# Loading the first norm's gain as one row, with a stream of zeros through TensorE while the tokens load

## The chip, the cores and the metric

The kernel runs on one core of a Trainium2 chip. The metric is device time in microseconds of one launch, as the median over runs. A core has five engines with queues of their own: TensorE (PE in the profile, its weight loads PEld), VectorE (DVE), ScalarE (ACT), GpSimd (POOL) and SyncE (SP), which issues the loads here.

## The reference

A decoder trunk of two layers on 256 tokens of width 1024, fp32. Each layer is a half-step SwiGLU feed-forward block, a token mixer (RWKV-7 in the first layer, sliding-window attention in the second), and another half-step feed-forward block, with a norm before and after each.

```python
def rms_norm(x, g):
    y = x * lax.rsqrt(jnp.mean(x * x, axis=-1, keepdims=True) + RMS_EPS)
    return y * g

def swiglu(x, w_in, w_out):
    gate, up = jnp.split(x @ w_in, 2, axis=-1)
    return (jax.nn.silu(gate) * up) @ w_out

for layer in range(DEPTH):
    g = norm_g[layer]
    h = h + 0.5 * rms_norm(swiglu(rms_norm(h, g[0]), ffn_w_in[layer, 0], ffn_w_out[layer, 0]), g[1])
    ...
```

The change concerns the very first step, `rms_norm(h, g[0])` of layer 0, and with it the first 36 us or so.

## The kernel before

Tokens lie on partitions in two blocks of 128, `self.h[0]` and `self.h[1]`, each 128x1024. A product with fp32 weights is made of three products in a reduced format (`mm3`, L226): the weight chunk (`wr`, 128x1024, 512 KB) is cast to a high part by ScalarE (L195), VectorE subtracts to get the low part (L201), and both lie in `W`. The activations are split the same way (`split`, L313): high part on ScalarE (L314), low part on VectorE (L315), into `xtl` (features 0 to 511) and `xth` (512 to 1023).

The start, in the order of the program:

- SP issues the load of `h[0]` (L89), of the identity (`cst`, L91), then the gain of the first norm (`gain`, L157): the row of 1024 values is read 128 times, once for each partition, 512 KB in all. Then comes the first weight chunk, `h[1]`, and more chunks. Four buffers `wr` hold raw chunks.
- For each token block, `hstat` (L285) squares the block on ScalarE (L290), `rstd` (L235) makes the factor r on VectorE (L239) and GpSimd (L242), `normed` (L294) multiplies the block with r and the gain in two halves of 512 on VectorE (L301), `transposed` (L305) turns each half with four TensorE transposes against the identity (L309), and `split` follows.
- `ffn_lead` then makes the first two blocks of the hidden layer from eight chunks (`w_in_lead`): 96 products of 512 columns, which show as L227. `ffn_main` streams the other weights (L362, L363, and L227 for the way down).

PSUM is used by banks of 128x512: six of them rotate as `bk` (`bank`), two as `bt` (`tbank`). The pools `t4` (four buffers of 128x1024) and `g2k` (fourteen of 128x512) rotate as well.

The program is written in the order above, but the order on each engine's queue comes from a scheduler that works with estimated durations; only some stages are pinned by hand. So at the start, seven products of the first token block stand ahead of the second block's transposes.

Of the kernel before, what the change touches and what calls it, by code (L numbers as in the profile page):

```python
# [16 lines left out]
P = 128  # L17
# [10 lines left out]
R_NORM = {}  # L28
# [49 lines left out]
class Trunk:  # L78
# [215 lines left out]
    def normed(self, i, r, g, xn):  # L294
        nc = self.nc
        for n in range(2):
            sl = slice(n * 512, n * 512 + 512)
            if g is None:
                nc.vector.tensor_scalar(xn[:, sl], self.h[i][:, sl], r, None, op0=ALU.mult)
            else:  # L300
                nc.vector.scalar_tensor_tensor(xn[:, sl], self.h[i][:, sl], r, g[:, sl],  # L301
                                               op0=ALU.mult, op1=ALU.mult)
        return xn

# [282 lines left out]
    def tm_core(self):  # L587
# [35 lines left out]

        acc0, todo = v_half(0, xv)
        run(todo)
        self.mix(xkm[:, :, toks[1]], 2, toks[1])
        self.tm_lora(1)
# [549 lines left out]
        for i in range(2):  # L1177
            unit.update({f"m{i}": merge(i), f"t{i}": bk_turn(i), f"y{i}": rows(i), f"bias{i}": gn_bias(i),
                         f"gate{i}": gn_gate(i), f"gn{i}": normed(i), f"yt{i}": turned(i), f"o{i}": out_proj(i),
                         f"c{i}0": chain(i, 0), f"c{i}1": chain(i, 1)})  # L1180
# [289 lines left out]
    def run(self, out):  # L1470
        nc, a = self.nc, self.a
        self.out = out
        self.tm_open()
        self.open("xt")
        self.open("sh0")
        self.tl("sh0", [P, 24])
        self.open("W1", 3)
        self.open("t4", 4)
        self.open("g2k", 14)
        self.tm_begin()  # L1480
        self.open("l1", side="right")
        self.open("W2", 5, side="right")
        self.turns = ["W1", "W2", "W2", "W1", "W2", "W2", "W1", "W2"]

        self.ffn_begin(0, None, 2, 3)
        g_pre = self.gain(R_NORM[(0, 0)])
        self.lead_chunk(0, 0)
        nc.sync.dma_start(self.h[1], a["x"][P:T, :])
        self.xt = xt = self.new_xt("xt")
        for i in range(2):  # L1490
            self.to_xt(i, self.hstat(i), [(g_pre, xt)])
        self.ffn_lead((0, 1))
        self.ffn_main()
        self.load(self.cols, a["cols"], self.mid)
        self.load(self.small, a["small"].to_broadcast([P, 272]), self.mid)
        self.load(self.cst[:, P:], a["consts"][:, P:], self.mid)
        self.tm_consts()
        g_post = self.gain(R_NORM[(0, 1)], self.mid)
        for i in range(2):
            self.tm_in(i, self.post(i, self.ffn_tail(i), g_post, True))  # L1500
        accs, g_post = self.tm_core()

        g_pre = self.gain(R_NORM[(0, 4)])
        xt = self.new_xt("xt")
        for i in range(2):
            self.to_xt(i, self.post(i, accs[i], g_post, False), [(g_pre, xt)])
        self.ffn_begin(1, xt)
        self.plan = list(P1)
        for i in range(2):
            self.ffn_lead((i,))  # L1510
        self.ffn_main()
        g_post = self.gain(R_NORM[(0, 5)], self.mid)

        self.kv_open()
        xt = self.new_xt("xt")
        xe = self.new_xt("ux", ("u", "xx"))
        self.plan = list(PKV)
        self.wkv = [self.stream(a["w_kv"][c], gains=C_GKV + 2 * c) for c in range(3)]
        for i in range(2):
            self.to_xt2(i, self.post(i, self.ffn_tail(i, self.early(i, TX1)), g_post, True), xe, xt)  # L1520
        self.ffn_begin(2, xt, 1)
        for i in range(2):
            self.kv(i, xe)
            self.ffn_lead((i,))
        self.ffn_main()
        self.att_region()
        self.ffn_main()
        g_post = self.gain(R_NORM[(1, 5)], self.mid)
        for i in range(2):
            self.post_last(i, self.ffn_tail(i), g_post)  # L1530
        for p in reversed(self.psum):
            p.release()
        self.close("W3", "W2", "ux", "kvp", "t4", "pad", "qT", "W1", "g2k", "sh2", "xt")
# [88 lines left out]
```

## Time and profile before

| what | value |
|---|---|
| median of three runs | 1058.08 us (1057.75 to 1059.89) |
| profiled execution | 1058.52 us |
| its span, first to last instruction | 1056.7 us |
| TensorE busy | 1027.6 us, 97% of the span |
| VectorE busy | 699.5 us, 66% |
| ScalarE busy | 565.3 us, 53% |
| mean granted TensorE clock | 0.996 |
| bytes read from HBM | 180.94 MB |

Busy time is the time in which the engine had work, not the time at its peak. In the lists, a line gives its start, its length, the engine, the source line, the tiles as out<-in, the shape, and in brackets how long the engine had stood idle and what ended that. A span of several instructions is merged into one line with their count (x7).

The row of the slices that gives the clock granted to TensorE shows full clock in every slice from the first on, also where no product had run yet; for the start, the pace of TensorE's own instructions says more.

### The profile page before, as it was taken

To read this page: it belongs to the slowest core of one execution; us is meant where nothing else is said; L and a number is where in the kernel's file an instruction comes from. 1 tells how busy PE (TensorE), PEld (TensorE's weight loads), DVE (VectorE), ACT (ScalarE), POOL (GpSimd) and SP (SyncE) were. 2 spreads that over 40 slices of the span, in tenths; PEclk is the share of its full clock that TensorE was granted. 3 is DMA by queue.
4 is the path that set the end of the run, shared out by engine and by line. 5 is a ranking of instruction groups with operands and counts; after the bars stand their busy time and mean duration, and the time that the engine had idled before them with its cause. 6 is when DMAs were issued, how large, how long until landed. Compare 5 with 4: busy or idle time off the path is not lost.

```text
span 1056.7 us, 16152 instructions
## 1 busy us (share of the span) xinstructions
PE 1027.6 (97%) x6264; PEld 859.3 (81%) x6264; DVE 699.5 (66%) x1125; ACT 565.3 (53%) x1014; POOL 20.5 (2%) x34
## 2 busy tenths in 40 slices
PE   6999999999999999999999999999999979999997
PEld 5888888779967887888888788888877758888885
DVE  6766655527798977766665676666658876765652
ACT  6654554355244546655455665455556755655541
POOL 0000000000000001000000000000010000000000
PEclk9999999999999999999999999999999999999999
DMA  8868665034354346766563376675535127766621
GB/s 285 248 187 279 220 193 165 23 117 141 120 167 135 122 134 207 258 199 206 194 182 122 116 268 212 209 237 189 180 104 175 41 94 254 237 214 196 183 78 40
DMA packets 52668, 183.04 MB, mean 173 GB/s; under 512 B 5744, under 2 KB 6000, under 8 KB 52464
## 3 DMA queue, kind: packets, MB, share of 16 engines
q1 hardware_dynamic: 52304, 181.49, 53.4%
q8 instruction: 49, 0.80, 0.3%
q10 hardware_dynamic: 288, 0.52, 0.1%
q14 instruction: 27, 0.22, 0.1%
HBM read 180.94 MB, written 1.05 MB: 172 GB/s over the span
## 4 chain that ended last, share of the span: by engine, by line
PE 91%; ACT 3%; DVE 3%; DMA 1%; issue 1%; POOL 0%; SPq 0%; DVEq 0%; POOLq 0%; ACTq 0%
PE bk L227 36%; PE bt L362 13%; PE bk L362 13%; PE bt L363 7%; PE bk L363 7%; PE bk L571 3%; PE bk L617 2%; PE bk L581 1%; PE bt L309 1%; PE bc L1002 1%; PE bk L1053 1%; ACT W L195 1%; PE bk L1397 1%; ACT g2k L1368 1%; DVE t L259 0%
## 5 line engine op out<-in xcount | busy, mean ns | idle before, releaser
L201 DVE TENSOR_TENSOR W<-wr,W 128x1024 fp32r<-128x1024 f32 x280 | 341.2, 1225 | 192.8 <-ACT W L195 191.9
L195 ACT CAST W<-wr 128x1024 fp32r<-128x1024 f32 x280 | 291.8, 1050 | 190.7 <-issue 96.5
L227 PE MATMUL bk<-W,g2k 128*128 128x512 f32 x1056 | 250.7, 394 | 0.0
L227 PEld LDWEIGHTS bk<-W,g2k 128*128 128x128 f32 x1056 | 196.1, 188 | 44.1
L362 PE MATMUL bk<-xtl,W 128*128 128x512 f32 x296 | 104.8, 392 | 0.0
L362 PE MATMUL bt<-xth,W 128*128 128x512 f32 x296 | 104.6, 391 | 0.0
L362 PE MATMUL bt<-xtl,W 128*128 128x512 f32 x296 | 104.4, 391 | 0.0
L362 PE MATMUL bk<-xth,W 128*128 128x512 f32 x296 | 104.4, 391 | 0.0
L363 PE MATMUL bt<-xth,W 128*128 128x256 f32 x296 | 83.3, 281 | 0.0
L363 PE MATMUL bk<-xth,W 128*128 128x256 f32 x296 | 83.2, 281 | 0.0
L363 PE MATMUL bk<-xtl,W 128*128 128x256 f32 x296 | 83.2, 281 | 0.0
L363 PE MATMUL bt<-xtl,W 128*128 128x256 f32 x296 | 83.1, 281 | 0.0
L227 PE MATMUL bk<-W,xtl 128*128 128x512 f32 x216 | 60.4, 427 | 6.4 <-ACT W L195 3.5
L362 PEld LDWEIGHTS bt<-xtl,W 128*128 128x128 f32 x296 | 55.6, 188 | 12.3 <-DVE xtl L350 0.5
L362 PEld LDWEIGHTS bk<-xtl,W 128*128 128x128 f32 x296 | 55.6, 188 | 12.2
L362 PEld LDWEIGHTS bk<-xth,W 128*128 128x128 f32 x296 | 55.6, 188 | 11.9
L362 PEld LDWEIGHTS bt<-xth,W 128*128 128x128 f32 x296 | 55.5, 188 | 11.8
L227 PEld LDWEIGHTS bk<-W,xtl 128*128 128x128 f32 x216 | 42.0, 200 | 20.0 <-ACT W L195 4.0
L363 PEld LDWEIGHTS bk<-xtl,W 128*128 128x128 f32 x296 | 55.9, 189 | 1.4
L363 PEld LDWEIGHTS bt<-xth,W 128*128 128x128 f32 x296 | 55.8, 189 | 0.1
L363 PEld LDWEIGHTS bt<-xtl,W 128*128 128x128 f32 x296 | 55.8, 189 | 0.1
L363 PEld LDWEIGHTS bk<-xth,W 128*128 128x128 f32 x296 | 55.8, 189 | 0.0
(287 smaller groups left out, 1375.7 us busy)
## 6 DMA issues: line engine op xcount, KB each, us to landing
wr<-in_w_in_dram SPq DMA_DIRECT2D x148, 512.0 KB, 3.8
wr<-in_w_out_dram SPq DMA_DIRECT2D x88, 512.0 KB, 3.6
wr<-in_w_in_lead_dram SPq DMA_DIRECT2D x28, 512.0 KB, 4.2
wr<-in_w_v_dram SPq DMA_DIRECT2D x16, 512.0 KB, 3.9
gain<-in_rows_dram SPq DMA_DIRECT2D x13, 512.0 KB, 4.5
wr<-in_w_k_dram SPq DMA_DIRECT2D x8, 512.0 KB, 4.0
wr<-in_w_r_dram SPq DMA_DIRECT2D x8, 512.0 KB, 3.5
wr<-in_w_o_dram SPq DMA_DIRECT2D x8, 512.0 KB, 4.3
```

Of the source, the lines that this page charges most:

```text
L195: self.follow(nc.scalar.copy(w[:, 0, :], raw), 0)
L201: self.follow(nc.vector.tensor_tensor(w[:, 1, :], raw, w[:, 0, :], op=ALU.subtract), 1)
L227: mm = lambda *x, **y: self.nc.tensor.matmul(*x, **y, **kw)
L309: t = self.nc.tensor.transpose(b[:, k * P:(k + 1) * P], xn[:, c:c + P], self.ident)
L362: mm(banks[j], hi[:, c0:c0 + P], xt[c][:, :, k4, :], start=(k == 0), stop=False)
L363: use[0] = mm(banks[j][:, 0:T], lo[:, c0:c0 + P], xt[c][:, 0, k4, :], start=False, stop=(k == KT - 1))
L571: self.nc.tensor.matmul(b[:, j * T:(j + 1) * T], ws[k // 4][:, c0:c0 + P], xf[:, k, :], start=(k == 0), stop=(k == KT - 1))
L581: nc.tensor.matmul(bs[j], l[:, k, j * P:(j + 1) * P], x[:, k, sl], start=(k == 0 and not e), stop=(k == KT - 1 and e == 1))
L617: mm(acc, x[:, 2 * k2 + k, :], w[:, k, :], start=(k2 + k == 0), stop=(k2 + k == 4))
L1002: mm(b[r, m * N:(m + 1) * N], W[r, v - hh * 16, :], XV[r, v, :], start=True, stop=True)
L1053: mm(out[hh][half[1 - e], m * N:(m + 1) * N], lhs, UV[part][:, hh * 16 + q, :], start=(not i and part == 0 and m == 0), stop=(part == e), ...
L1368: nc.scalar.activation(S[x], S[x], AF.Exp, bias=st[:, 1, x:x + 1], accum_out=st[:, 3, x:x + 1])
```

## The change

The gain of the first norm is loaded as a single row of 4 KB onto one partition. TensorE spreads it: a row of 128 ones as the stationary operand and the gain's row as the moving one give, in two products of 512 columns with one row of contraction, the gain on all 128 partitions, in two PSUM banks. `normed` then reads it from PSUM. Ahead of these two products stand five products of a 128x512 tile of zeros with itself, whose result nothing reads. The tiles for zeros and ones are set by VectorE.

```diff
-                nc.vector.scalar_tensor_tensor(xn[:, sl], self.h[i][:, sl], r, g[:, sl],
+                nc.vector.scalar_tensor_tensor(xn[:, sl], self.h[i][:, sl], r, g[n] if isinstance(g, list) else g[:, sl],
                                                op0=ALU.mult, op1=ALU.mult)
...
         self.ffn_begin(0, None, 2, 3)
-        g_pre = self.gain(R_NORM[(0, 0)])
+        zero, one, row = self.g2k([P, 512]), self.g2k([P, 512]), self.t4()
+        nc.vector.memset(zero, 0.0)
+        nc.vector.memset(one[0:1, 0:P], 1.0)
+        nc.sync.dma_start(row[0:1, :], a["rows"][R_NORM[(0, 0)]:R_NORM[(0, 0)] + 1, :])
+        busy = self.tbank()
+        for _ in range(5):
+            nc.tensor.matmul(busy, zero[:, 0:P], zero, start=True, stop=True)
+        g_pre = [self.bank() for _ in range(2)]
+        for n in range(2):
+            nc.tensor.matmul(g_pre[n], one[0:1, 0:P], row[0:1, n * 512:n * 512 + 512], start=True, stop=True)
         self.lead_chunk(0, 0)
         nc.sync.dma_start(self.h[1], a["x"][P:T, :])
```

## The prediction

> **What bounds the kernel now.** I read the page first, then TensorE's waits, the chain of waits over the first 16 us, and the timeline there, engine by engine.
>
> The page: the span, TensorE's line, and the shares of the chain that ended last.
>
> ```profile
> span 1056.7 us, 16152 instructions
> PE 1027.6 (97%) x6264; PEld 859.3 (81%) x6264; DVE 699.5 (66%) x1125; ACT 565.3 (53%) x1014; POOL 20.5 (2%) x34
> PE 91%; ACT 3%; DVE 3%; DMA 1%; issue 1%; POOL 0%; SPq 0%; DVEq 0%; POOLq 0%; ACTq 0%
> ```
>
> TensorE is busy nearly throughout, so what an earlier start saves should reach the end unless some later wait eats it. Its waits (total, times, longest):
>
> ```profile
> PE bt L309 <- DVE t L301: 7.7, 1, 7.7
> PE bk L227 <- ACT W L195: 3.5, 2, 1.8
> ```
>
> The largest is the start: 7.7 us until the first normed half block. The chain of waits there (start, length, what):
>
> ```profile
> 1.65 5.13 DMA gain<-in_rows_dram
> 6.92 0.76 DVE t L301
> 7.73 1.97 PE bt L309 x8
> 9.70 3.86 PE bk L227 x7
> 13.56 0.74 PE bt L309 x4
> 14.31 0.59 ACT xtl L314
> ```
>
> The gain lands at 1.65 + 5.13 = 6.78 and releases the first normed half. The timeline of the other engines (start, length):
>
> ```profile
> 4.44 0.63 ACT L290 ACTIVATE t<-h 128x512 f32<-128x512 f32 x1 [2.42 <-DMA h<-in_x_dram]
> 6.05 0.56 POOL L242 TENSOR_TENSOR rs<-rs,mhalf 128x1 f32<-128x1 f32 x1 [4.28 <-DVE rs L239]
> 8.09 1.05 ACT L195 CAST W<-wr 128x1024 fp32r<-128x1024 f32 x1 [2.32 <-DMA wr<-in_w_in_lead_dram]
> 9.05 0.58 ACT L314 CAST xtl<-bt 128x512 fp32r<-128x512 f32 x1
> 9.17 1.23 DVE L201 TENSOR_TENSOR W<-wr,W 128x1024 fp32r<-128x1024 f32 x1 [0.83 <-ACT W L195]
> 10.76 0.57 ACT L314 CAST xth<-bt 128x512 fp32r<-128x512 f32 x1
> 11.36 0.69 DVE L315 TENSOR_TENSOR xth<-bt,xth 128x512 fp32r<-128x512 f32 x1 [0.30 <-ACT xth L314]
> 11.97 1.41 DVE L301 SCALAR_TENSOR_TENSOR t<-h,rs,gain 128x512 f32<-128x512 f32 x2
> 13.29 2.36 DVE L201 TENSOR_TENSOR W<-wr,W 128x1024 fp32r<-128x1024 f32 x2
> ```
>
> The factor r is known at 6.05 + 0.56 = 6.61, so the gain is only 0.3 us later than r. But its 512 KB also stand ahead of the first weight chunk, whose cast (8.09) holds ScalarE until 9.05. TensorE's rows (PEld is a weight load, one for each product):
>
> ```profile
> 8.00 1.29 PEld L309 LDWEIGHTS bt<-cst,t 128*128 128x128 f32 x6
> 11.65 1.19 PEld L227 LDWEIGHTS bk<-W,xtl 128*128 128x128 f32 x3
> 14.95 1.45 PEld L227 LDWEIGHTS bk<-W,xtl 128*128 128x128 f32 x7 [0.48 <-ACT xtl L314]
> 15.29 0.19 PEld L227 LDWEIGHTS bk<-W,xtl 128*128 128x128 f32 x1
> 18.31 2.50 PE L227 MATMUL bk<-W,xtl 128*128 128x512 f32 x10
> 205.82 1.98 PEld L581 LDWEIGHTS bk<-xx,l 128*128 128x128 f32 x17
> ```
>
> Pitch, from start to start: products (1.19 - 0.33) / 2 = 0.43 us before 13 us, with 0.33 the length of the last load, against (2.50 - 0.40) / 9 = 0.233 later; 128-column fp32 work (1.29 - 0.23) / 5 = 0.21 in the transposes at 8 us against (1.98 - 0.19) / 16 = 0.11 later. So TensorE runs at half pace until about 14 us. From 15.29 to 36 us it doesn't wait; before that it does. The third product after the restart, at 15.29, is my yardstick: all later work follows it closely.
>
> **The change, part by part.** The sum is against the profiled execution, 1058.52 us (span 1056.7 plus 1.8 around it), 0.44 above the median 1058.08.
>
> One row for a spread load. SP issues the same number of loads. Removed are 512 KB between the constants and the first chunk. The row of the trace nearest to a small load there is the constants':
>
> ```profile
> 1.18 0.42 SPq L91 DMA_DIRECT2D cst<-in_consts_dram  x1
> cst<-in_consts_dram SPq DMA_DIRECT2D x1, 64.0 KB, 3.4
> ```
>
> They land at 4.6. The row of 4 KB lands at 4.6 at the earliest and, as the gain, at 6.8 at the latest; I take 4.7, since it is far smaller than the constants. The first chunk, 1.3 us behind the gain before (8.09 - 6.78), comes at 5.9 to 6.8, and its cast ends by 7.9, out of the way of the first split.
>
> The zero stream and the spreading, all ahead of the transposes in TensorE's queue. Prices:
>
> ```profile
> L617 PE MATMUL bk<-wr,xv x32: 592/592/595, 207.8 to 306.2; 128*128 128x512 f32 x32
> 207.83 2.74 PE L617 MATMUL bk<-wr,xv 128*128 128x512 f32 x6
> L95 DVE MEMSET mhalf<- 128x1 f32 x1 | 0.1, 59 | 0.8 <-PEq L1611 0.8
> L301 DVE SCALAR_TENSOR_TENSOR t<-h,rs,gain x8: 743/748/753, 6.9 to 406.0; 128x512 f32<-128x512 f32 x8
> L1354 DVE SCALAR_TENSOR_TENSOR g2k<-bk,cst 128x512 f32<-128x512 f32 x12 | 8.0, 683 | 0.8 <-PE bk L1348 0.8
> ```
>
> An fp32 product of 512 columns has a pitch of (2.74 - 0.59) / 5 = 0.43 us at full pace and, doubled like the others, 0.86 at half pace. A memset of 128x512 isn't in the trace: it lies between 0.06 (the one-column memset) and 0.75 (a two-input pass of that size); I take 0.6, nearer the latter, for it has the same elements. VectorE is idle then, and its first memset is at 0.8. So the stream starts at 1.5 (0.95 to 1.65). All at half pace: five products to 5.8, the first spread half to 6.65 and, with 0.2 to drain, ready at 6.85; the second at 7.7. If the clock rises on the way, both come before r. VectorE's halves began at 6.92 and 7.6: the first now starts between 6.65 and 6.85, I take 6.75. Reading the gain out of PSUM costs 0.68 against 0.75 by the rows above, which I set at nothing.
>
> The clock. Its records in this execution also show one slow stretch late in the kernel (busy time of PE, PEld, DVE, ACT, POOL with counts, granted clock, DMA share, GB/s):
>
> ```profile
> 867.30:874.10 6.80, 5.66 (x13) 4.09 (x14) 5.60 (x7) 4.51 (x5) 0.00 (x0) 0.50 0.49 180
> 858.51 2.39 PEld L227 LDWEIGHTS bk<-W,xtl 128*128 128x128 f32 x11 [1.07 <-DVE W L201]
> 869.24 5.79 PEld L227 LDWEIGHTS bk<-W,xtl 128*128 128x128 f32 x16 [0.97 <-DVE W L201]
> ```
>
> It followed idle stretches. At the start the slow pace held for 6 us of broken work (7.73 to about 14). Zeros from 1.5 to 7.7 are unbroken, so I take full pace at the transposes. The Trainium skill ("TensorE: Matmul & The Clock Gate", Part 1) says that the gate opens after one busy window of about 3.4 us and that the windows run free of the program. The slow stretch of 6.8 us is two such windows, so the trace agrees on the length. By that rule an estimate puts the rise between 4.9 and 8.3 us, and in the late part of it the four transposes would cost 0.4 us more than in my sum.
>
> The sum. Transposes of the first four tiles: 6.75 + 0.75 + 0.05 + 3 x 0.11 + 0.3 to drain = 8.2, when ScalarE's first split starts (9.05 before, 0.85 earlier). From there the old distances hold: the second split (10.76 to 9.9), VectorE's low part (11.36 to 10.5), the second block's norm (11.97 to 11.1), the low part of chunk 1 (13.29 to 12.4, done by 13.66). TensorE gets its products of the first block behind it at 0.23 each and waits for the second block: transposes at 11.1 + 0.75 + 0.05 = 11.9, split 12.6 to 13.2, restart 13.2; the yardstick product waits for chunk 1's low part, 13.7. That is 1.6 earlier than 15.29. Weighted down a little for the late clock and the late second half: 1.5 us.
>
> Is it kept? Behind the yardstick the weights have room:
>
> ```profile
> 17.89 2.54 DVE L201 TENSOR_TENSOR W<-wr,W 128x1024 fp32r<-128x1024 f32 x2
> 24.87 5.08 PEld L227 LDWEIGHTS bk<-W,xtl 128*128 128x128 f32 x22
> ```
>
> The first low part of the second lead block is ready at 19.1 and needed at 24.87, so 1.5 us more demand is covered. The two PSUM banks held by the gain and the buffers taken at the start (two of fourteen, one of four) are covered as well: the lead needs four banks of six, and the zeros are read out by 6 us. If that cover were gone, the flush would wait for the second block's norm, long over by 36 us. So I take the 1.5 us to the end: 1058.5 - 1.5 = 1057.0 for the execution profiled, 1056.6 against the median.
>
> **The rivals.**
>
> No early clock: zeros don't raise it, or the row lands as late as 6.8. With transposes at 0.21 (0.4 later) and the second block's at half pace as well, the restart comes at 14.0 and the yardstick at 14.8, a gain of 0.5: 1057.6. For it: nothing in the trace shows zeros as operands. Against: in the rows above the pace follows how long TensorE has been busy, and zeros keep it busy as other numbers do.
>
> More than forecast: the loads come 1.3 to 2.2 us earlier, and with the second block's tokens at 7.2 to 8.1 instead of 9.3 its squares may be ordered before the first split, so that its norm runs 0.6 earlier and the weights' low parts with it: gain 2.2 to 2.5, 1055.7. For it: engine order here isn't program order (seven products stand before the second block's transposes at 13.35). Against: nothing forces a new order.
>
> Slower: the row arrives late. 4 KB onto one partition is a form of load that the trace doesn't show. TensorE's queue then stands still at the spreading, and all transposes behind it. It decides from a landing at 7.7 on: with 0.43 for the spreading and 0.2 to drain, the first half then starts at 8.3, 1.5 later than I take, and the gain is used up. Were it to land behind the first chunk and the second block's tokens and three more chunks (five loads at 1.3 from 4.6, so 11.1), the first half would start at 11.7, 5.0 later than I take: 1056.6 + 5.0 = 1061.6. Against it: every load of the start landed in the order of issue.
>
> **How the numbers follow.** Forecast 0.54; no early clock 0.17; more than forecast 0.20; late row 0.05; a new order later in the kernel that costs one chunk's cast and split (1.05 + 1.23 = 2.3, more than the gain) 0.04. About 0.2% (2.1 us) is what a measurement of this kernel can tell. Faster by over that: the second rival and a few hundredths of the forecast's upper end, 0.26; slower: 0.08; same: 0.66. The range runs from 1054.8 (gain 2.5, and some of the slow stretch at 867 falling away: its 16 loads at (5.79 - 0.19) / 15 = 0.37 against 0.22 are worth 2.3) to 1058.5 (no gain, 0.4 of spread). The forecast's own range is 1055.8 to 1057.4.
>
> **What would show it.** In the changed profile: five fp32 products from 1.5 us, first and second half norm at about 6.75 and 7.5 released by TensorE or r and no longer by a load; transposes at a pitch of 0.11; the first chunk's cast before 7; the restart near 13.2; TensorE's first product of the main part 1.5 earlier. Wrong if the transposes still run at 0.21, if the norm waits for the spreading beyond 7.2, or if TensorE's later waits (855 to 869 above all) have grown.

## The result: 0.8% slower, lost in the first 44 us

| | before | after |
|---|---|---|
| median | 1057.91 us (4 runs, 1056.80 to 1059.89) | 1066.96 us (4 runs, 1065.01 to 1069.11) |
| profiled execution, its span | 1058.52, 1056.7 | 1065.01, 1063.2 |
| first product of the main part (L362) | 36.2 | 43.6 |

The ratio is 1.0081, with a 95% interval of 1.0059 to 1.0104. I had forecast 1056.6, with 1058.5 as the upper end. The busy line of the page, kernel after:

```profile
PE 1036.1 (97%) x6278; PEld 862.8 (81%) x6278; DVE 699.6 (66%) x1127; ACT 565.3 (53%) x1014; POOL 20.6 (2%) x34
```

TensorE has 14 instructions more, though the diff adds seven products, and VectorE two (the memsets). Where the time went is read from the rows of the main part's first line (shortest, median and longest duration, then the first and the last start), of the kernel before and the kernel after:

```profile
L362 PE MATMUL bk<-xtl,W x296: 389/390/477, 36.2 to 1019.0; 128*128 128x512 f32 x148
L362 PE MATMUL bt<-xtl,W x296: 390/390/503, 43.6 to 1031.1; 128*128 128x512 f32 x148
```

The main part starts 7.4 us later, and the span is 6.5 longer. So the loss is made in the first 44 us. TensorE's waits after (total, times, longest) hide it, for the row of the start there is:

```profile
PE bt L309 <- DVE t L301: 3.0, 1, 3.0
```

The wait for the first normed half fell from 7.7 to 3.0, only because TensorE was busy with the zeros and the spreading in the meantime. The timeline of the start, kernel after:

```profile
1.48 6.98 PE L1492 MATMUL bt<-g2k 128*128 128x512 f32 x10 [1.48 <-DVE g2k L1487]
5.99 0.56 POOL L242 TENSOR_TENSOR rs<-rs,mhalf 128x1 f32<-128x1 f32 x1 [4.22 <-DVE rs L239]
7.76 1.04 ACT L195 CAST W<-wr 128x1024 fp32r<-128x1024 f32 x1 [2.05 <-DMA wr<-in_w_in_lead_dram]
8.39 1.98 PE L1495 MATMUL bk<-t,g2k 1*128 1x512 f32 x4
8.84 1.23 DVE L201 TENSOR_TENSOR W<-wr,W 128x1024 fp32r<-128x1024 f32 x1 [2.93 <-ACT W L195]
10.41 0.16 DVE L239 SCALAR_TENSOR_TENSOR rs<-hs 128x1 f32<-128x1 f32 x1 [0.34 <-ACT t L290]
11.39 1.22 DVE L201 TENSOR_TENSOR W<-wr,W 128x1024 fp32r<-128x1024 f32 x1 [0.82 <-ACT W L195]
12.53 1.40 DVE L301 SCALAR_TENSOR_TENSOR t<-h,rs,bk 128x512 f32<-128x512 f32 x2
13.33 1.11 PE L309 MATMUL bt<-cst,t 128*128 128x128 f32 x4 [2.96 <-DVE t L301]
15.12 1.22 PE L227 MATMUL bk<-W,xtl 128*128 128x512 f32 x2 [0.68 <-ACT xtl L314]
27.85 0.60 PE L309 MATMUL bt<-cst,t 128*128 128x128 f32 x4
```

Three things are to be seen. First, ten zero instructions and four spreading ones end at 10.37, where I had seven. Second, r is known at 6.55 (6.61 before) and the gain is spread by 10.37, but VectorE starts the norm at 12.53: ahead of it on its queue now stand the low parts of two chunks (8.84, 11.39) and the second block's statistics (10.41). Before, the norm (6.92) stood ahead of the first of these splits (9.17). Third, TensorE's work from 13.33 on is broken by waits and runs at half pace: four transposes take 1.11, against 0.60 for the last four at 27.85. Before, all sixteen were over ahead of the product at 15.29.

The chain of waits of the first 20 us says the same from the other end (start, length, what), kernel after; before, it ran through the gain and then TensorE:

```profile
2.42 6.60 DMA h<-in_x_dram
...
9.04 1.34 ACT t L290 x4
...
13.19 0.74 DVE t L301
13.93 1.14 DVE W L201
...
18.17 1.11 PE bt L309 x4
```

The start is now set by the second block's tokens and their squares, and by VectorE, where normed halves and weight splits alternate.

### The profile page after: what moved, and what is told of

It is laid out like the page before. It is cut to its first block, busy times and chain, and to the rows that moved or that the text cites. A ratio compares the mean times of both kernels' runs of the same rounds, so it can differ in the third digit from the quotient of the medians.

```text
span 1063.2 us, 16179 instructions
## 1 busy us (share of the span) xinstructions
PE 1036.1 (97%) x6278; PEld 862.8 (81%) x6278; DVE 699.6 (66%) x1127; ACT 565.3 (53%) x1014; POOL 20.6 (2%) x34
## 4 chain that ended last, share of the span: by engine, by line
PE 92%; ACT 3%; DVE 3%; DMA 1%; issue 1%; POOL 0%; SPq 0%; DVEq 0%; POOLq 0%; ACTq 0%
PE bk L227 37%; PE bt L362 13%; PE bk L362 13%; PE bk L363 7%; PE bt L363 7%; PE bk L571 3%; PE bk L617 2%; PE bk L581 1%; PE bt L309 1%; ACT W L195 1%; PE bc L1002 1%; PE bk L1053 1%; DMA h<-in_x_dram 1%; PE bk L1397 1%; ACT g2k L1368 1%
## 5 line engine op out<-in xcount | busy, mean ns | idle before, releaser
L362 PE MATMUL bk<-xtl,W 128*128 128x512 f32 x296 | 104.8, 392 | 0.0
L362 PE MATMUL bt<-xth,W 128*128 128x512 f32 x296 | 104.6, 391 | 0.0
L362 PE MATMUL bt<-xtl,W 128*128 128x512 f32 x296 | 104.5, 392 | 0.0
L362 PE MATMUL bk<-xth,W 128*128 128x512 f32 x296 | 104.4, 391 | 0.0
L362 PEld LDWEIGHTS bt<-xtl,W 128*128 128x128 f32 x296 | 55.6, 188 | 12.2 <-DVE xtl L350 0.4
L362 PEld LDWEIGHTS bk<-xtl,W 128*128 128x128 f32 x296 | 55.6, 188 | 12.1
L362 PEld LDWEIGHTS bk<-xth,W 128*128 128x128 f32 x296 | 55.6, 188 | 11.9
L362 PEld LDWEIGHTS bt<-xth,W 128*128 128x128 f32 x296 | 55.5, 188 | 11.8
```

The lines of the kernel that those rows point to most:

```text
L362: mm(banks[j], hi[:, c0:c0 + P], xt[c][:, :, k4, :], start=(k == 0), stop=False)
```

## The experiments

My theory: the scheduler put the first ~30 instructions of each engine in another order, and that order costs the time; the zeros and the spreading by themselves cost little. Rivals: the late spreading, the zeros, the slow clock, or a late load cost it directly.

To part order from work, I wrote the start as a list of steps and held TensorE, VectorE and ScalarE to it for both token blocks and the eight lead chunks. L loads a chunk, H loads the second block's tokens, Q squares, R makes r, N is a normed half, C a chunk's cast, S its low part, T transposes, X and Y the high and low part of the tokens, P products; the first digit is the block or chunk. With the gain's and the zeros' instructions left aside, the first list below gives the order of the kernel before on these three engines, and the second that of the kernel after. No run holds the engines to the order of before and changes nothing else; that holding them costs nothing by itself is seen from row_no_zeros and zeros_alone, whose main parts start at 36.0 and 36.6. In these kernels `normed` shows as L449, the split as L457 and L459, the chunk's cast and low part as L461 and L463, the products as L428, zeros as L1559 or L1560, the spreading as L1563.

```
before: L0 H0 L1 L2 L3 Q0 R0 N00 N01 C0 T00 T01 S0 L4 X00 Y00 Q1 R1 X01 Y01 P06 C1 P01 N10 N11 T10 T11 ...
after:  L0 H0 L1 L2 L3 Q0 R0 C0 S0 L4 Q1 R1 C1 S1 L5 C2 C3 N00 N10 S2 L6 N01 N11 S3 L7 T00 X00 ...
```

All runs together; "main" is the first start of L362 in the profiled execution (36.2 before), "norm" the first start of the normed halves (6.92 before). The runs were made in three groups (the first four rows, the next four, the last three), in which the median of before was 1058.43, 1058.22 and 1058.61 (29 runs each). The ratio is worked out from the single runs and is not the quotient of the two medians; the two can differ (zeros_free_order: 1.0054 against 1.0036).

| run | gain | zero products | order | median (runs) | ratio, 95% interval | norm | main |
|---|---|---|---|---|---|---|---|
| order_alone | 512 KB | 0 | of after | 1065.84 (6) | 1.0068, 1.0052 to 1.0084 | 12.94 | 43.4 |
| order_of_before | row | 5 | of before | 1060.03 (12) | 1.0015, 1.0000 to 1.0030 | 9.31 | 37.2 |
| row_no_zeros | row | 0 | of before | 1058.85 (12) | 1.0016, 0.9991 to 1.0040 | 6.97 | 36.0 |
| zeros_alone | 512 KB | 3 | of before | 1058.26 (12) | 1.0004, 0.9990 to 1.0018 | 7.32 | 36.6 |
| order_clock_held | 512 KB | 11 | of after | 1072.01 (4) | 1.0119, 1.0077 to 1.0162 | 12.93 | 44.2 |
| row_other_queue | row, ScalarE's queue | 0 | of before | 1057.48 (12) | 0.9982, 0.9965 to 1.0000 | 6.67 | 35.0 |
| row_other_queue_1 | row, ScalarE's queue | 1 | of before | 1058.56 (12) | 1.0012, 0.9988 to 1.0036 | 6.62 | 34.9 |
| row_free_order | row | 0 | scheduler's | 1062.46 (10) | 1.0028, 1.0012 to 1.0045 | 6.84 | 39.2 |
| one_split_ahead | 512 KB | 0 | of before, one step moved | 1060.44 (12) | 1.0010, 0.9995 to 1.0024 | 10.36 | 38.7 |
| zeros_free_order | 512 KB | 5 | scheduler's | 1062.38 (12) | 1.0054, 1.0032 to 1.0075 | 6.93 | 40.3 |
| row_other_queue_2 | row, ScalarE's queue | 0 | of before | 1058.87 (12) | 1.0000, 0.9986 to 1.0014 | 6.62 | 35.3 |

**order_alone**: the kernel before, with the order of after and nothing else.

```diff
-  ... Q0 R0 N00 N01 C0 T00 T01 S0 L4 X00 Y00 Q1 R1 X01 Y01 ...
+  ... Q0 R0 C0 S0 L4 Q1 R1 C1 S1 L5 C2 C3 N00 N10 S2 L6 N01 N11 S3 ...
```

> The kernel before, unchanged in what it computes and loads (gain as 512 KB, no zeros, no spreading), but with the order of VectorE, ScalarE and TensorE at the start pinned to that of the changed kernel: the first norm stands behind two chunk splits and the second block's statistics on VectorE. Theory ORDER (most of the 9 us is the new order, and the cold clock that follows from it): 6 us or more slower than before, 1064 or above, first norm at 12 to 13 us. Theory LATE SPREAD (most of it is the gain that comes out of TensorE at 9.6 instead of 6.8): nothing comes out of TensorE here, so at most 2 us slower, 1060 or below.

Four rows of its timeline, and the row of the main part:

```profile
9.26 1.23 DVE L463 TENSOR_TENSOR W<-wr,W 128x1024 fp32r<-128x1024 f32 x1 [3.20 <-ACT W L461]
11.79 1.23 DVE L463 TENSOR_TENSOR W<-wr,W 128x1024 fp32r<-128x1024 f32 x1 [0.82 <-ACT W L461]
12.94 1.41 DVE L449 SCALAR_TENSOR_TENSOR t<-h,rs,gain 128x512 f32<-128x512 f32 x2
13.74 1.11 PE L309 MATMUL bt<-cst,t 128*128 128x128 f32 x4 [13.74 <-DVE t L449]
L362 PE MATMUL bt<-xtl,W x296: 390/390/496, 43.4 to 1030.6; 128*128 128x512 f32 x148
```

The gain lies ready long before, and there is no zero and no spreading, yet the norm waits behind the two splits and the main part starts at 43.4, 7.2 of the 7.4 us later. This shows that the order is enough for nearly all of the loss at the start; in the medians it is 7.4 of the 9.05 us. 6.0 of the 7.2 are there already at the first transposes (13.74 against 7.73 before), ahead of anything that TensorE's pace could do.

**order_of_before**: the whole change, held to the order of before (`pinned` emits the steps, `in_order` holds the three engines to them).

```diff
 # the diff of the change, and
+        self.pinned(g_pre, xt, """L0 H0 L1 L2 L3 Q0 R0 N00 N01 C0 T00 T01 S0 L4 X00 Y00 ...""")
+        self.in_order(first, "PE", "DVE", "Activation")
```

> The whole change (row, five zero products, two spreading products), but with the order of VectorE, ScalarE and TensorE at the start pinned to that of the kernel before. ORDER: the norm starts when the first spread half is ready, 9.6 us, 2.7 later than before, some of it given back by the clock that is then at full pace: 1.0 to 2.5 us slower than before, 1059 to 1060.5. LATE SPREAD: 5 us slower or more, 1063 or above.

Its timeline:

```profile
8.07 1.98 PE L1563 MATMUL bk<-t,g2k 1*128 1x512 f32 x4
9.31 1.53 DVE L449 SCALAR_TENSOR_TENSOR t<-h,rs,bk 128x512 f32<-128x512 f32 x2 [3.30 <-PE bk L1563]
10.11 1.44 PE L309 MATMUL bt<-cst,t 128*128 128x128 f32 x8
```

Here the norm does wait for the spreading: VectorE idles 3.30 us for it and starts at 9.31, 2.4 later than before. The eight transposes then run at full pace (1.44 for eight; before, 1.97), TensorE makes up for part of it, and the main part starts 1.0 later. So in this order the zeros and the late spreading cost 1.0 (not a share of the 7.4, of which the order alone makes 7.2), and the median is 1.6 us above before, an interval that just touches no change.

**row_no_zeros** and **zeros_alone**: the two halves of the change, each in the order of before.

```diff
 # row_no_zeros
-        for _ in range(5):
-            nc.tensor.matmul(busy, zero[:, 0:P], zero, start=True, stop=True)
 # zeros_alone: 512 KB gain, and
+        for _ in range(3):
+            nc.tensor.matmul(busy, zero[:, 0:P], zero, start=True, stop=True)
```

> The row and the two spreading products without the zeros, order of the kernel before. Two products of two instructions at half pace, 3.4 us from 4.7 us on, are ready at 6.6 (first half) and 8.3 (second): first norm at 6.9 and 8.4 against 6.9 and 7.6. If the removed 512 KB bring the other loads forward as predicted (first chunk landed at 5.9 to 6.8): 0 to 0.7 us faster. If they don't (7.7, as in the changed kernel): 0 to 1 us slower than before.

> The gain as 512 KB as before, with three zero products (six instructions, 1.5 to about 6.6 us) ahead of the transposes, order of the kernel before. If zeros raise the clock and the clock matters: transposes at a pitch of 0.11 from 7.7, yardstick product 0.7 to 1.5 earlier than 15.3, 1056.4 to 1057.3. If the clock falls back before the products or the start is bound by ScalarE and VectorE alone: same as before within 0.4.

Neither differs measurably from before. In row_no_zeros the row is there at 4.81, but its four instructions take 3.75 us at half pace, and the first chunk's cast starts at 8.21 (8.09 before), so that nothing comes earlier (rows of its timeline):

```profile
4.81 3.75 PE L1563 MATMUL bk<-t,g2k 1*128 1x512 f32 x4 [4.81 <-DMA t<-in_rows_dram]
8.21 1.05 ACT L461 CAST W<-wr 128x1024 fp32r<-128x1024 f32 x1 [2.55 <-DMA wr<-in_w_in_lead_dram]
```

In zeros_alone the clock is up at the transposes (eight from 8.12 on take 1.38, against 1.97 before), and is lost again. Windows of zeros_alone (start:end, length, busy time and count of PE, PEld, DVE, ACT and POOL, granted clock, DMA share, GB/s):

```profile
7.40:10.80 3.40, 1.78 (x9) 1.02 (x9) 2.46 (x3) 2.21 (x5) 0.00 (x0) 1.00 1.02 418
10.80:14.20 3.40, 3.25 (x8) 2.35 (x9) 3.10 (x7) 2.92 (x5) 0.56 (x1) 0.50 0.90 322
```

Behind 3.4 us with TensorE busy for only 1.78 stand 3.4 us at 0.50. Full pace early was not kept through the waits of this run's start.

**order_clock_held**: order_alone with 11 zero products, to keep the clock up to the late transposes.

```diff
+        for _ in range(11):
+            nc.tensor.matmul(busy, zero[:, 0:P], zero, start=True, stop=True)
```

> The order of the changed kernel again with the gain as 512 KB, but eleven zero products (22 instructions, 1.5 to about 13.5 us) keep TensorE busy until the late transposes, so that the clock is at full pace from there on. If part of the 7 us is the half pace after the idle wait (ORDER with CLOCK): the first product of the main part comes 1.3 to 2.0 earlier than the 43.4 of the pinned order alone, 1063.8 to 1064.5. If the order alone makes it (waits on VectorE and ScalarE): 43.2 to 43.5 and about 1065.8 as there.

This one missed: the main part starts at 44.2, later than either case allowed. The clock was up at the first transposes (four in 0.60), but waits follow, and half pace comes back for 6.8 us. A row of its timeline, a window of the start, and a window from far behind it:

```profile
13.87 0.60 PE L309 MATMUL bt<-cst,t 128*128 128x128 f32 x4
17.50:24.30 6.80, 5.71 (x16) 4.66 (x17) 6.77 (x8) 3.14 (x5) 0.00 (x0) 0.50 0.81 245
345.20:369.00 23.80, 23.80 (x262) 20.02 (x262) 12.90 (x17) 8.93 (x17) 0.00 (x0) 0.50 0.14 44
```

So the run can't tell how much of the 7 us is order alone and how much is half pace that the order's waits bring with them, beyond the 6.0 that order_alone shows ahead of the first transposes. The last row is a second stretch at half pace, far from the start, in work that the edit doesn't touch. This execution (1076.72, the slowest of four) started its main part 8.0 us later than before and has a span 18.2 longer, so some 10 us were lost behind the start; why the stretch came, and what made the other three (1066.64 to 1075.63), wasn't traced.

**row_other_queue**, **row_other_queue_1**, **row_other_queue_2**: the row is issued on ScalarE's queue, beside the first load of SP, in the order of before; the second has one zero product, the third repeats the first.

```diff
-        nc.sync.dma_start(row[0:1, :], ...)
+        nc.scalar.dma_start(row[0:1, :], ...)
```

> As the row without zeros and with the order of the kernel before, but the row is issued from ScalarE's queue at 0.7 us and not between the constants and the first chunk on SP's. If the row in SP's queue is what held the first chunk at 8.2: chunk at 5.9 to 6.9. If the early loads are slow whatever stands there: chunk at 7.5 to 8.2 again. Spreading starts about 3 to 3.5 instead of 4.8, so both halves of the gain are ready by 7 us, first norm at 6.65 and 7.3: main part starts at 34.8 to 35.7 against 36.2 (before), 1057 to 1058, or the same as before if ScalarE's wait for the first chunk decides.

> The same with one zero product ahead of the spreading (two instructions, 1.5 to 3.2 us), so that TensorE is busy from 1.5 to about 7 and the clock rises before the transposes (pitch 0.11): 0.3 to 0.8 faster than without; main part at 34.3 to 35.3, 1056.5 to 1057.5. If the clock falls back in the waits for the first products, as it did with three zeros ahead of the old load: same as without.

> The same kernel as row_other_queue once more (row of 4 KB issued from ScalarE's queue, no zeros, before's order), to see whether its small gain of 0.2% stands: ratio 0.997 to 1.000 if it is the 1.2 us by which its main part started earlier (35.03 against 36.19), 0.999 to 1.002 if the late stretches at half pace decide the median.

Two rows of the timeline of the first of them, then one of row_other_queue_1:

```profile
3.24 3.75 PE L1563 MATMUL bk<-t,g2k 1*128 1x512 f32 x4 [3.24 <-DMA t<-in_rows_dram]
7.43 1.04 ACT L461 CAST W<-wr 128x1024 fp32r<-128x1024 f32 x1 [1.62 <-DMA wr<-in_w_in_lead_dram]
7.42 1.97 PE L309 MATMUL bt<-cst,t 128*128 128x128 f32 x8 [0.16 <-DVE t L449]
```

The spreading is off the path, r sets the norm, the first chunk comes 0.7 earlier and the main part starts 1.2 earlier (1.3 with one zero product, the best start of all). The first run gave 0.9982, the repetition 1.0000: what is 1.2 us at the start can't be told from no change at the end. The profiled executions show how wide the spread is: of the same kernel, one ended at 1057.77 with a mean granted clock of 0.996, the other at 1061.65 with 0.992, with main parts that started 0.3 apart. No version here beats the kernel before by more than a measurement can tell.

On the clock the expectation of row_other_queue_1 missed. TensorE had been busy from 1.48 to 7.27 and idle for 0.16 us ahead of the transposes, yet these eight took 1.97, the half pace of before; in the kernel after, zeros alone had doubled the pace by 6.58. Two thirds of this run's busy time were the spreading's products with one row of contraction; whether these count for less no run here tests.

**row_free_order** and **zeros_free_order**: each half of the change in the order that the scheduler gives it.

```diff
 # row_free_order: the change without its 5 zero products; zeros_free_order: before, and
+        for _ in range(5):
+            nc.tensor.matmul(busy, zero[:, 0:P], zero, start=True, stop=True)
```

> The change without the zeros, order left to the scheduler. ORDER: it puts one half of the first norm before the first chunk's split and the rest of the norms ahead of the second chunk's, so the first norm isn't held behind two splits: 0 to 2.5 us slower than before, 1058 to 1060.5, far from the 1067 of the change. LATE SPREAD: the spreading itself is the loss and the zeros add little: 1063 or above.

> The kernel before with the five zero products alone (gain by 512 KB, no spreading), in the order that the scheduler gives it: norm of the first block, then the first split, as before; only small moves behind it (the second block's factor ahead of the second half's low part). If the order costs and the zeros do not: ten zero instructions end at about 8.5, the transposes start there instead of at 7.7, at the full pace, and the main part starts at 36.2 to 37.2; time within 0.15% of before. Rival (the zeros by themselves cost what the change cost): main part at 40 or later, time over 1062.

Four rows of the timeline of row_free_order, then five of zeros_free_order:

```profile
7.68 1.22 DVE L201 TENSOR_TENSOR W<-wr,W 128x1024 fp32r<-128x1024 f32 x1
8.83 0.74 DVE L301 SCALAR_TENSOR_TENSOR t<-h,rs,bk 128x512 f32<-128x512 f32 x1
9.35 1.05 ACT L195 CAST W<-wr 128x1024 fp32r<-128x1024 f32 x1
10.30 0.58 ACT L314 CAST xtl<-bt 128x512 fp32r<-128x512 f32 x1
```

```profile
8.20 1.04 PE L309 MATMUL bt<-cst,t 128*128 128x128 f32 x8
9.41 0.63 ACT L290 ACTIVATE t<-h 128x512 f32<-128x512 f32 x1 [0.24 <-DMA h<-in_x_dram]
10.68 1.04 ACT L195 CAST W<-wr 128x1024 fp32r<-128x1024 f32 x1
11.63 0.58 ACT L314 CAST xtl<-bt 128x512 fp32r<-128x512 f32 x1
12.27 0.74 PE L227 MATMUL bk<-W,xtl 128*128 128x512 f32 x2 [3.03 <-ACT xtl L314]
```

With the row alone, the main part starts 3.2 later than in row_no_zeros, which does the same work, and the kernel is slower than before. Its 1062.46 lies above the 1058 to 1060.5 that I expected of ORDER and just below LATE SPREAD's 1063; but the same spreading stands in row_no_zeros, so the order makes the difference. The weight split between the two normed halves (7.68) costs little: in row_no_zeros the second half waits for its gain and starts at 8.60, against 8.83 here. The orders part behind it. ScalarE has the second block's squares and the second chunk's cast (9.35) ahead of the first split, which comes at 10.30 against 9.65 in row_no_zeros, and VectorE has the second block's norm and the second chunk's split ahead of the first low part, which comes at 12.76 against 10.43. Which of these steps makes the 3.2 wasn't tested.

With the zeros alone my expectation failed. I had looked at VectorE's order, which hardly moves, and overlooked ScalarE's: the transposes are done by 9.24, but the second block's squares (9.41) and the second chunk's cast (10.68) stand ahead of the first split, which comes at 11.63 against 9.05 before. TensorE waits 3.03 us for it. The numbers of that expectation's rival, that zeros cost by themselves, came true (40.3, 1062.38), but not its reason: zeros_alone and order_of_before stream zeros too, and their main parts start within 1.0 us of before. So each half of the change moves the order; 3.0 and 4.1 us against 36.2 come near to the 7.4 of both, though the orders differ.

**one_split_ahead**: the kernel before with one step of one engine moved.

```diff
-  ... Q0 R0 N00 N01 C0 T00 T01 S0 L4 X00 ...
+  ... Q0 R0 C0 S0 L4 N00 N01 T00 T01 X00 ...
```

> The kernel before (512 KB gain, no zeros, its order on every engine), with one thing moved: on VectorE the low part of the first chunk (L201, 1.23 us) stands ahead of the first block's two normed halves instead of behind them. Order theory: VectorE then waits for that chunk's load and cast (9.14 before) and the norm starts at about 10.4 instead of 6.92, the first transposes at 11.1 instead of 7.73, and the main part's first product (36.19 before) comes 2 to 3.5 us later, 38.2 to 39.7; time 1060 to 1062. Rival (the cost in the changed kernel comes from the second block's statistics and the second split standing ahead too, or from the clock, and one split alone is absorbed): main part by 37.0, time within 0.1% of before.

Its timeline:

```profile
9.21 1.23 DVE L463 TENSOR_TENSOR W<-wr,W 128x1024 fp32r<-128x1024 f32 x1 [3.35 <-ACT W L461]
10.36 1.41 DVE L449 SCALAR_TENSOR_TENSOR t<-h,rs,gain 128x512 f32<-128x512 f32 x2
```

One split of 1.23 us ahead of the norm makes VectorE wait for a load (3.35 idle) and moves the norm by 3.4 and the main part by 2.5, as expected. The median is 1.8 us above before; the ratio's interval still holds no change, so at the end this is inconclusive.

## Why the prediction was wrong

- **The order, the step that failed.** "From there the old distances hold" carried the order of before over into the changed kernel. The order was made anew, and that is 7.2 of the 7.4 us (order_alone). The second rival saw that a new order could come, but took it for a gain and held against it that "nothing forces a new order"; a new order that costs stood at 0.04, and late in the kernel. What made the scheduler choose it, which estimate of which instruction, stays open; the runs show only that each half of the change sets off a new order.
- **The price of an fp32 product, mis-sized by two.** I read a pitch of 0.43 us as that of one product. It is that of one of its two instructions. Zeros and spreading end at 10.37 and not at 7.7. The trace of before held the answer, in a row of a line with four products in the code (two token blocks, two halves), where it counts eight:

```profile
L659 PE MATMUL bk<-gain,hwa x8: 591/592/595, 224.7 to 227.7; 65*128 65x512 f32 x8
```

  The Trainium skill ("FP8 and Floating Point Precision", TensorE Precision Notes) gives four passes through the array for a true fp32 product; at the 0.233 us of a reduced-format product that would be an estimate of 0.93, and the trace has 2 x 0.43 = 0.86. In the order of before this error costs 2.4 us at the norm and 1.0 at the main part (order_of_before).
- **The clock: right, then lost.** The zeros raise it. The starts of the weight loads, kernel after, go from 0.85 apart to 0.43:

```profile
5.06 0.34 PEld L1492 LDWEIGHTS bt<-g2k 128*128 128x128 f32 x1 [0.52 <-issue]
5.91 0.34 PEld L1492 LDWEIGHTS bt<-g2k 128*128 128x128 f32 x1 [0.52 <-issue]
6.58 0.19 PEld L1492 LDWEIGHTS bt<-g2k 128*128 128x128 f32 x1 [0.33 <-issue]
7.01 0.19 PEld L1492 LDWEIGHTS bt<-g2k 128*128 128x128 f32 x1 [0.24 <-issue]
13.10:23.40 10.30, 8.42 (x25) 6.32 (x26) 10.07 (x13) 6.45 (x8) 0.00 (x0) 0.51 0.71 222
```

  That falls inside the 4.9 to 8.3 of my estimate. But the transposes came at 13.33, behind 2.96 us of waiting, and the last row, a window, shows 0.51 from 13.1 to 23.4. With the order of before they did run at full pace.
- **The loads.** The row came when I said: in row_free_order and row_no_zeros TensorE starts on it at 4.69 and 4.81 (4.7 forecast). The first chunk mostly did not: against a forecast of 5.9 to 6.8 its cast starts at 7.76 after and 8.21 in row_no_zeros, and at 6.61 only in row_free_order. Against the 8.09 of before, taking away 512 KB ahead of it gained from nothing to 1.5 us; why it varies so stays open.
- **Is it kept.** A start that is 7.4 later gives a span 6.5 longer, and 7.2 gives 6.1 (order_alone), so a loss was kept nearly whole. That a gain is kept isn't shown: 1.2 us at the main part were not to be found in the median.
- **The profiled execution and the median.** The change costs 6.5 us in the profiled executions and 9.05 in the medians. The profiled execution of after was the fastest of its four; the others had a lower mean granted clock (0.989 to 0.991 against 0.993). Where they lost it wasn't traced.

## What to carry to other kernels

Where a scheduler orders the queues, a change that adds work to one engine can reorder the others: set the order of instructions on every engine, not only the one that you look at, beside the old one before pricing anything, and pin it where it should stay. Check the count of a row against the products in the code before using its duration as the price of a product. Work that fills an engine's wait need not buy anything; here with the order held, three zero products and five cost little and gained nothing.

## What the runs showed of the hardware

- Zeros count as work for the clock: pitch 0.85 to 0.43 us within 6.6 us of the launch's first instruction, with operands of zero only.
- The clock falls without a whole idle window: in zeros_alone a stretch of 3.4 us with TensorE busy for 1.78 was followed by 3.4 at half pace. Of the 1.78, 1.38 are transposes; whether these count like products no run here tells. The Trainium skill ("TensorE: Matmul & The Clock Gate", Part 1) ties the fall to at least one idle window of about 3.4 us; the length agrees, the idleness doesn't.
- The windows' granted clock shows 1.00 at a start whose pitch is that of half pace, so there the rows must be read, not that column:

```profile
1.50:6.30 4.80, 4.80 (x6) 2.17 (x7) 0.22 (x2) 1.85 (x5) 0.58 (x2) 1.00 0.80 221
```

- A memset of 128x512 on VectorE took 0.48 us, less than the 0.60 that I took for it.
